# State chain of an RWKV-7 trunk layer: the solve's products on four 64 by 64 tiles and two PSUM banks, and the output norm's squares summed as two rounded parts

## The chip, the cores and the metric

One NeuronCore of one Trainium2 chip runs the whole kernel. The metric is the device time of one execution in microseconds (us), the median over several executions. Engine names are those of the profile: PE is TensorE's matmul stream, PEld its weight loads, DVE is VectorE, ACT is ScalarE, POOL is GpSimd, SP is SyncE, which here only issues DMAs.

## The reference

One layer of a hybrid decoder trunk over 1024 tokens of width 1024. The part that the change touches is the RWKV-7 branch: a recurrence over the tokens with one 64 by 64 state per head (16 heads), and a norm of its output per head.

```python
def rwkv7_scan(r, w, k, v, kk_neg, kk_a):
    def step(state, inp):
        rt, wt, kt, vt, an, bn = inp
        sa = jnp.einsum('bhvk,bhk->bhv', state, an)
        state = state * wt[:, :, None, :] + sa[..., None] * bn[:, :, None, :] + vt[..., None] * kt[:, :, None, :]
        yt = jnp.einsum('bhvk,bhk->bhv', state, rt)
        return state, yt
    ...
# in rwkv_branch:
    mu = jnp.mean(y, axis=-1, keepdims=True)          # over the 64 channels of a head
    var = jnp.mean(jnp.square(y - mu), axis=-1, keepdims=True)
    y = ((y - mu) * lax.rsqrt(var + LNX_EPS)).reshape(B, S, RWKV_WIDTH)
    y = y * ln_x_w.astype(f32) + ln_x_b.astype(f32)
    bonus = jnp.sum(rh * kh * r_k.astype(f32), axis=-1, keepdims=True) * vh
    y = y + bonus.reshape(B, S, RWKV_WIDTH)
    return y.astype(dt) * g
```

Around it stand one combined input projection, a pooling branch, cross-attention, three sigmoid gates that merge the branches, an output projection and a convolutional feed-forward layer.

## The kernel before

Everything is held with channels on the 128 partitions and tokens along the free axis. Large matrix products run as three passes over rounded parts: a float32 operand is split into a rounded high part (`fp32r`) and the rest, and `mm3` (lines 180 to 182) multiplies high by high, high by low and low by high, each a 128x128 weight against 128x512. Products of plain float32 operands are recorded as two passes each.

The recurrence is cut into 16 chunks of 64 tokens (`NCH = 16`, `C = 64`); the preceding stage solves each chunk's triangular system in 32 by 32 blocks and leaves the chunk's matrices in DRAM. The function `chain` then walks the chunks in order. Two heads stand on the 128 partitions (`lo` is partitions 0 to 63, `up` is 64 to 127), eight such pairs `i` make up the 16 heads. A chunk `c` has three visits to PE, and between them values go through DVE and ACT:

1. `pr`: 16 products of the state and the chunk's matrices, 64 columns each. DVE copies the result to `Rs` (line 800).
2. `py<-ring` (part of the output) and `pu`: `pu = nt * Rs` is the solve's product, 16 products of 64x64 by 64x64, head `lo` on rows and columns 0 to 63 and head `up` on 64 to 127, all into one bank. DVE copies the lower half of `pu` into `hv` (line 809) and ACT the upper half (line 810).
3. `ph` (the new state's increment) and `py<-rb` (the rest of the output), which read `hv`. DVE adds `ph` and the decayed state `Hd` into the next chunk's `hv` (line 828, two additions: `lo`, `up`), then into `Hn` (line 833); eight small ACT instructions scale `Hn` by the decay into `Hd` (line 835). ACT copies the output `py` out (line 836).

The next chunk's `pr` waits for both additions of line 828, so the chunks form one chain.

To keep PE busy while that chain passes through DVE and ACT, `visit` first emits *fill*: further steps of the input projection for the pooling, query and gate columns, three passes per step (`psg<-hh`). The table `fills`, here `279 + 121 * (v - 1) // 46`, says how many steps stand before visit `v`: two or three between any two visits. The scheduler orders each engine's instructions; `later` adds pure ordering between them.

Each block `b` of two chunks has 1024 by 128 outputs in `y`. `outputs(b - 1, n, ...)` finishes half of the block before, four channel groups at a time: squares on ACT (line 714), a sum over each head's 64 channels by one float32 product with a block matrix of ones (`pvar`, line 716), logarithm and exponential on ACT for the inverse root (`rstd`, line 214), and four DVE products and sums: by the inverse root, by `ln_w`, plus `gt[0]`, times `gt[1]` (lines 720 to 723). `gt[0]` and `gt[1]` are loaded from DRAM for each block by `gate`, and `store` writes the block. SP issues these and the loads of the next block's matrices (`ring`, `hv`, `pair`, `bk`, `rb`) from one queue.

PSUM has eight banks: the fill uses `psg` with tag `g1` (two), `psg` with tag `g0` (two) is idle in the chain, `py` and `pvar` share `pss` (two), and `bank` hands out `psc` and `psk` in turn to `pr`, `pu` and `ph`.

Of the kernel before, what the change touches and what calls it, by code (L numbers as in the profile page):

```python
# [9 lines left out]
F32 = mybir.dt.float32  # L10
FR = mybir.dt.float32r
AF = mybir.ActivationFunctionType
ALU = mybir.AluOpType
# [4 lines left out]
P = 128  # L18
# [3 lines left out]
C = 64  # L22
# [22 lines left out]
def trunk_kernel(ctx: ExitStack, tc: tile.TileContext, xT, memT, pvec, w_in, w_kv, w_upd, w_upg,  # L45
                 w_pool, w_ppool, w_pmem, w_prwkv, w_o, w_fup, w_fdn, out):
    nc = tc.nc
    V, A, G, PE, SP = nc.vector, nc.scalar, nc.gpsimd, nc.tensor, nc.sync
# [3 lines left out]
    psg = ctx.enter_context(tc.tile_pool(name="psg", bufs=2, space=PSUM))  # L52
# [11 lines left out]
    d_g = dtile([8, P, T], "d_g")  # L64
    d_bv = dtile([8, P, T], "d_bv")
# [23 lines left out]
    bonesr = const.tile([P, P], FR, name="bonesr")  # L89
# [5 lines left out]
    bones = bonesr.bitcast(F32)  # L95
# [122 lines left out]
    def rstd(dst, ps, eps_col, scale=1.0):  # L218
        act(dst, ps, AF.Ln, bias=eps[:, eps_col:eps_col + 1], scale=scale)
        act(dst, dst, AF.Exp, scale=-0.5)  # L220

    def later(i, ins, plain=False):

        tc.add_manual_dep(i if plain else i.ins, ins.name, nosync, reason="order")
# [13 lines left out]
    for k in range(KC):  # L238
        tag = ("X01", "X11", "HV", "HV")[k // 2]
# [116 lines left out]
    lr = lr_ctx.enter_context(tc.tile_pool(name="lr", bufs=1, side="right"))  # L356

    ld = lr.tile([P, T], FR, name="ld", tag="ld")
# [333 lines left out]
            dst = dst[:, :, n]  # L692
        SP.dma_start(dst.rearrange("c p t -> p c t"), src.rearrange("p (c u) s -> p c (u s)", u=2))

    gates, ready_y = {}, {}

    def gate(b):

        gates[b] = []
        for src, e in ((d_bv, "ld"), (d_g, "la")):  # L700
            gates[b].append(lr.tile([P, 8, 2 * C], F32, name="gt", tag=e))
            SP.dma_start(gates[b][-1], src[:, :, b * 2 * C:(b + 1) * 2 * C].rearrange("n p t -> p n t"))

    def store(b):

        SP.dma_start(d_y[:, :, b * 2 * C:(b + 1) * 2 * C].rearrange("n p t -> p n t"), ready_y[b])

    def outputs(b, n, q, after):

        y, gt = ready_y[b], gates[b]  # L710
        ln_w = pv[:, PV["ln_w"][0]:PV["ln_w"][0] + 8]
        ns = slice(n, n + 4)
        y_, q_ = y[:, ns], q.rearrange("p (n t) -> p n t", t=2 * C)
        A.activation(q_, y_, AF.Square)
        ps = pss.tile([P, 512], F32, name="pvar", tag="s")
        m = PE.matmul(ps, bones, q, start=True, stop=True)  # L716
        if after is not None:
            later(m, after)
        rstd(q, ps, 2, 1.0 / 64)
        V.tensor_tensor(y_, y_, q_, op=ALU.mult)  # L720
        V.tensor_tensor(y_, y_, ln_w[:, ns].unsqueeze(2).broadcast_to([P, 4, 2 * C]), op=ALU.mult)
        V.tensor_tensor(y_, y_, gt[0][:, ns], op=ALU.add)
        V.tensor_tensor(y_, y_, gt[1][:, ns], op=ALU.mult)

    def chain(fills):

        lo, up = slice(0, 64), slice(64, 128)
        ring = rw.tile([P, 2, 8, 3, 2 * C], F32, name="ring", tag="AR")
        pair = rw.tile([P, 2, 2, 8, 2 * C], F32, name="pair", tag="HV")
        state = rw.tile([P, 4, 8, C], F32, name="Rs", tag="NT")  # L730
        Rs, Hn, Hd = (state[:, n] for n in range(3))
        root = state[:, 3].rearrange("p n t -> p (n t)")
        held = {}

        due = []

        def load(b):

            ar, nt = ring[:, b % 2], pair[:, b % 2, 0]
            hv = rw.tile([P, 2, 8, 2, C], F32, name="hv", tag=f"X{b % 2}2")  # L740
            rb = rw.tile([P, 8, 2, 2 * C], F32, name="rb", tag=f"X{b % 2}1")
            bk = rw.tile([P, 8, 2, P], F32, name="bk", tag=f"X{b % 2}0")
            due.extend([(ar, d_ar[b].rearrange("p g i e t -> p (g i) e t")),
                        (hv[up, 0], d_hv[b, up].rearrange("p g i (u s) -> p (g i) u s", u=2)),
                        (hv[lo, 1], d_hv[b, lo].rearrange("p g i (u s) -> p (g i) u s", u=2)),
                        (nt, d_nt[b].rearrange("p g i t -> p (g i) t")),
                        (bk, d_bk[b].rearrange("p g i u s -> p (g i) u s")),
                        (rb, d_rb[b].rearrange("p g i e t -> p (g i) e t"))])
            held[b] = ar, nt, hv, rb, bk, pair[:, b % 2, 1]

        def send(n, after=None):

            while due and n:
                i = SP.dma_start(*due.pop(0))
                if after is not None:
                    later(i, after)
                n -= 1

        turn = [0]

        def bank(name):
            turn[0] ^= 1
            return (psc if turn[0] else psk).tile([P, 8, C], F32, name=name, tag="c" if turn[0] else "k")

        visits = [0]

        def visit(products, after):

            wide = fill_to(fills(visits[0]))
            visits[0] += 1  # L770
            for n, ((out_, l, r), kw) in enumerate(products):
                m = PE.matmul(out_, l, r, **kw)  # L772
                if n == 0:
                    later(m, wide)
                if after is not None:
                    later(m, after)
                after = m.ins
            send(1, after)
            return after

        ready = None
        for b in range(2):
            load(b)
            send(6)
        for c in range(NCH):
            b, u = divmod(c, 2)
            if u == 0 and 0 < b < NCH // 2 - 1:
                load(b + 1)
            ar, nt, hv, rb, bk, y = held[b]
            t = slice(u * C, (u + 1) * C)  # L790
            once = dict(start=True, stop=True)
            pr = bank("pr")
            py = pss.tile([P, 8, C], F32, name="py", tag="s")
            ke, ko = (up, lo) if c == 0 else (slice(0, P), slice(0, P))
            row = []
            for i in range(8):
                row.append(((pr[up, i], ar[ko, i, 2, t], hv[ko, 1, i, u]), once))
                row.append(((pr[lo, i], ar[ke, i, 0, t], hv[ke, 0, i, u]), once))
            visit(row, ready)
            made = V.tensor_copy(Rs, pr).ins  # L800
            pu = bank("pu")
            row = []
            for i in range(8 if c else 0):
                kw = dict(start=i == 0, stop=False)
                row.append(((py[lo, i], hv[lo, 0, i, u], ar[lo, i, 1, t]), kw))
                row.append(((py[up, i], hv[up, 1, i, u], ar[up, i, 1, t]), kw))
            row += [((pu[q, i], nt[q, i, t], Rs[q, i]), once) for i in range(8) for q in (lo, up)]
            last = visit(row, made)
            V.tensor_copy(hv[lo, 0, :, u], pu[lo])
            ready = A.copy(hv[up, 1, :, u], pu[up]).ins  # L810
            row = []
            if c + 1 < NCH:
                ph = bank("ph")
                for i in range(8):
                    row.append(((ph[up, i], bk[:, i, u, 64:128], hv[:, 1, i, u]), once))
                    row.append(((ph[lo, i], bk[:, i, u, 0:64], hv[:, 0, i, u]), once))
            for i in range(8):
                kw = dict(start=c == 0 and i == 0, stop=i == 7)
                row.append(((py[lo, i], hv[:, 0, i, u], rb[:, i, 0, t]), kw))
                row.append(((py[up, i], hv[:, 1, i, u], rb[:, i, 1, t]), kw))  # L820
            visit(row, ready)
            if c + 1 < NCH:
                hx = held[(c + 1) // 2][2]
                for q, e in ((lo, 0), (up, 1)):
                    if c == 0:
                        ready = V.tensor_copy(hx[q, e, :, 1 - u], ph[q]).ins
                    else:
                        ready = V.tensor_tensor(hx[q, e, :, 1 - u], ph[q], Hd[q], op=ALU.add).ins
                if c + 2 < NCH:
                    if c == 0:  # L830
                        V.tensor_copy(Hn, ph)
                    else:
                        V.tensor_tensor(Hn, ph, Hd, op=ALU.add)
                    for i in range(8):
                        A.activation(Hd[:, i], Hn[:, i], AF.Identity, scale=Dc[:, i, c + 1:c + 2])
            A.copy(y[:, :, t], py)
            ready_y[b] = y
            if b:
                outputs(b - 1, 4 * u, root, last)
            if u:  # L840
                if b:
                    store(b - 1)
                gate(b)
        for n in (0, 4):
            outputs(b, n, root, None)
        store(b)

    fill = [(j, spilled(d_zp[j])) for j in range(4)] + [(4 + j, spilled(d_zq[j])) for j in range(4)]
# [927 lines left out]
    last = [half_down(1, 0)]  # L1776
# [75 lines left out]
```

## Time and profile before

| | |
|---|---|
| median of 3 runs | 1952.37 us (1947.69, 1952.37, 1952.64) |
| the profiled execution | 1947.9 us, of which the span of its instructions is 1946.2 us |
| granted TensorE clock in it | 0.993 |
| busy share of the span | PE 97%, DVE 70%, ACT 54%, POOL 40% |
| the state chain | first `pr` at 666.0 us, the last chunk's `py` at 861.7 us |

The page counts the time in which an engine had an instruction running. A matmul's end is modelled, so matmul records overlap: a pass of the fill is recorded as 0.39 us but the next one starts about 0.23 us later, and what a group of passes costs PE is read from the starts. Rows of the time line merge neighbouring instructions of one kind; `x32` behind a group of small products are 16 products of two passes each. In brackets stands how long the engine had been idle, and what ended that.

### The profile page before, as it was taken

To read this page: it belongs to the slowest core of one execution; us is meant where nothing else is said; L and a number is where in the kernel's file an instruction comes from. 1 tells how busy PE (TensorE), PEld (TensorE's weight loads), DVE (VectorE), ACT (ScalarE), POOL (GpSimd) and SP (SyncE) were. 2 spreads that over 40 slices of the span, in tenths; PEclk is the share of its full clock that TensorE was granted. 3 is DMA by queue.
4 is the path that set the end of the run, shared out by engine and by line. 5 is a ranking of instruction groups with operands and counts; after the bars stand their busy time and mean duration, and the time that the engine had idled before them with its cause. 6 is when DMAs were issued, how large, how long until landed. Compare 5 with 4: busy or idle time off the path is not lost.

```text
span 1946.2 us, 33744 instructions
## 1 busy us (share of the span) xinstructions
PE 1886.9 (97%) x12204; PEld 1522.7 (78%) x12204; DVE 1356.7 (70%) x2022; ACT 1046.1 (54%) x2158; POOL 784.1 (40%) x867
## 2 busy tenths in 40 slices
PE   8999999999999999999999999999999999999997
PEld 6767777777777887778788888878788888888886
DVE  8677577677677345556964444679698888877798
ACT  7685385475474245455664344546554545454544
POOL 4422222222222211111323455556599889822441
PEclk9999999999999999999999999999999999999999
DMA  5326326335349669965336444653322222289775
GB/s 163 130 72 186 99 76 184 93 95 168 95 122 310 191 191 297 312 196 190 102 112 231 124 137 130 208 161 121 110 81 87 78 88 88 86 250 223 168 184 146
DMA packets 269639, 296.26 MB, mean 152 GB/s; under 512 B 18336, under 2 KB 219168, under 8 KB 266400
## 3 DMA queue, kind: packets, MB, share of 16 engines
q1 hardware_dynamic: 248480, 271.56, 44.8%
q0 software_dynamic: 11856, 14.16, 4.5%
q10 hardware_dynamic: 9136, 8.39, 1.4%
q8 instruction: 96, 1.57, 0.3%
q14 instruction: 71, 0.58, 0.1%
HBM read 207.00 MB, written 87.03 MB: 151 GB/s over the span
## 4 chain that ended last, share of the span: by engine, by line
PE 62%; DVE 5%; DMA 4%; issue 2%; ACT 2%; POOL 1%; ACTq 0%; POOLq 0%; DVEq 0%; SPq 0%
PE psg L180 10%; PE psg L182 10%; PE psg L181 10%; PE psf L182 6%; PE psf L180 6%; PE psf L181 6%; PE psd L181 2%; PE psd L182 2%; PE psd L180 2%; PE py L772 2%; PE pr L772 1%; DMA g<-d_zg 1%; PE ph L772 1%; PE pvar L716 1%; PE pu L772 1%
## 5 line engine op out<-in xcount | busy, mean ns | idle before, releaser
L139 POOL TENSOR_TENSOR wlo<-wraw,whi 128x256 fp32r<-128x256 f32 x464 | 403.0, 881 | 829.0 <-ACT whi L132 753.6
L180 PE MATMUL psg<-hh,whi 128*128 128x512 f32 x928 | 377.7, 407 | 12.4 <-ACT whi L132 9.0
L182 PE MATMUL psg<-hh,wlo 128*128 128x512 f32 x928 | 367.6, 397 | 1.8 <-POOL wlo L139 1.5
L181 PE MATMUL psg<-hl,whi 128*128 128x512 f32 x928 | 368.1, 397 | 0.7 <-DVE hl L266 0.6
L132 ACT CAST whi<-wraw 128x256 fp32r<-128x256 f32 x472 | 181.5, 403 | 246.8 <-PE psg L181 98.9
L180 PEld LDWEIGHTS psg<-hh,whi 128*128 128x128 f32 x928 | 174.8, 188 | 57.4 <-ACT whi L132 13.0
L182 PEld LDWEIGHTS psg<-hh,wlo 128*128 128x128 f32 x928 | 174.8, 188 | 44.1 <-POOL wlo L139 6.1
L181 PEld LDWEIGHTS psg<-hl,whi 128*128 128x128 f32 x928 | 175.0, 189 | 39.8 <-issue 4.3
L1178 POOL TENSOR_TENSOR wt<-a,wt 128x256 fp32r<-128x256 f32 x136 | 156.3, 1173 | 35.4 <-ACT wt L1177 35.2
L180 PE MATMUL psd<-f,u 128*128 128x512 f32 x292 | 113.3, 391 | 1.1 <-ACT f L1590 1.1
L181 PE MATMUL psd<-f,u 128*128 128x512 f32 x292 | 113.8, 390 | 0.5 <-DVE f L1594 0.5
L182 PE MATMUL psd<-f,u 128*128 128x512 f32 x292 | 113.6, 389 | 0.0
L182 PE MATMUL psf<-h2h,wt 128*128 128x512 f32 x272 | 105.9, 390 | 0.2 <-POOL wt L1178 0.2
L180 PE MATMUL psf<-h2h,wt 128*128 128x512 f32 x272 | 105.9, 389 | 0.1
L181 PE MATMUL psf<-h2l,wt 128*128 128x512 f32 x272 | 105.8, 389 | 0.0
L1192 DVE SCALAR_TENSOR_TENSOR d<-z,pv,d 128x1023 f32<-128x1023 f32 x68 | 101.1, 1491 | 2.2
L1178 POOL TENSOR_TENSOR wt<-s,wt 128x256 fp32r<-128x256 f32 x68 | 79.9, 1195 | 3.3 <-ACT wt L1177 2.0
L180 PE MATMUL psf<-t,wt 128*128 128x512 f32 x204 | 79.4, 389 | 0.0
L181 PE MATMUL psf<-t,wt 128*128 128x512 f32 x204 | 79.4, 389 | 0.0
L182 PE MATMUL psf<-t,wt 128*128 128x512 f32 x204 | 79.4, 389 | 0.0
L1190 ACT ACTIVATE d<-z,pv 128x1024 f32<-128x1024 f32 x34 | 42.4, 1248 | 65.8 <-DVE z L1272 50.1
L1177 ACT CAST wt<-a 128x256 fp32r<-128x256 f32 x136 | 50.7, 405 | 40.8 <-POOL wt L1178 28.1
(430 smaller groups left out, 4507.3 us busy)
## 6 DMA issues: line engine op xcount, KB each, us to landing
wraw<-in_w_in SPq DMA_DIRECT2D x176, 128.0 KB, 2.5
a<-in_w_fup SPq DMA_DIRECT2D x128, 128.0 KB, 2.4
d_ar<-AR SPq DMA_DIRECT2D x24, 512.0 KB, 4.2
d_zg<-st SPq DMA_DIRECT2D x48, 256.0 KB, 3.4
ring<-d_ar SPq DMA_DIRECT2D x8, 1536.0 KB, 10.8
wraw<-in_w_fup SPq DMA_DIRECT2D x80, 128.0 KB, 2.6
fraw<-d_f SPq DMA_DIRECT2D x33, 256.0 KB, 4.3
d_rb<-RB SPq DMA_DIRECT2D x16, 512.0 KB, 5.4
```

The source lines that it names most:

```text
L132: i = A.copy(hi, src)
L139: (V if lo_on_dve[0] else G).tensor_tensor(lo, src, hi.bitcast(F32), op=ALU.subtract)
L180: first = PE.matmul(ps, wh, xh, start=start, stop=False)
L181: PE.matmul(ps, wh, xl, start=False, stop=False)
L182: last_mm[0] = PE.matmul(ps, wl, xh, start=False, stop=stop).ins
L716: m = PE.matmul(ps, bones, q, start=True, stop=True)
L772: m = PE.matmul(out_, l, r, **kw)
L1177: A.copy(w[0][:, us], src[u])
L1178: low = eng.tensor_tensor(w[1][:, us], src[u], w[0][:, us].bitcast(F32), op=ALU.subtract)
L1190: A.activation(d, z, AF.Identity, scale=col("cw2", j), bias=col("cb", j))
L1192: V.scalar_tensor_tensor(d[:, n:], z[:, :T - n], col(cw, j), d[:, n:], op0=ALU.mult, op1=ALU.add)
```

## The change

Four things are changed in `chain` and its helpers.

- **The solve's products.** `pu` gets two banks instead of one (the next two turns of `bank`). Even `i` go to the first bank as before. For odd `i` the output half is swapped: head `lo` (rows 0 to 63) writes columns 64 to 127, head `up` writes columns 0 to 63, into the second bank. Four 64 by 64 tiles of the array are used in turn. DVE copies the first bank to `hv` in two copies of 64x256 (lines 820 and 821 of the changed kernel), ACT the second bank in two copies (lines 822 and 823).
- **The norm's sum.** `squared` makes the squares twice on ACT, once rounded into `sq[:, 0]` and once exactly into a PSUM tile `ysum`, and DVE subtracts to give the remainder `sq[:, 1]` (line 712). `outputs` sums them with two `fp32r` products (lines 722 and 725) instead of one float32 product. The inverse root stays in the PSUM tile.
- **Places.** The squares are written at the start of a chunk, and `outputs` between the copies of `pu` and the third visit, not at the end of the chunk. `Hn` moves from SBUF to a `psg` tile with tag `g0`, which `ysum` also uses.
- **Buffers.** `sq` takes the tag `ld` that held `gt[0]`; `gt[0]` takes the tag `la`, and `gt[1]` the part of `state` that held `Hn` and `root`. Hence it is printed as `Rs` in rows of the changed program.

```diff
     def gate(b):
-        gates[b] = []
-        for src, e in ((d_bv, "ld"), (d_g, "la")):
-            gates[b].append(lr.tile([P, 8, 2 * C], F32, name="gt", tag=e))
-            SP.dma_start(gates[b][-1], src[:, :, b * 2 * C:(b + 1) * 2 * C].rearrange("n p t -> p n t"))
+        gates[b] = lr.tile([P, 8, 2 * C], F32, name="gt", tag="la"), slot[0]
+        for gt, src in zip(gates[b], (d_bv, d_g)):
+            SP.dma_start(gt, src[:, :, b * 2 * C:(b + 1) * 2 * C].rearrange("n p t -> p n t"))
...
-    def outputs(b, n, q, after):
+    def squared(b, n, sq):
+        q = psg.tile([P, 512], F32, name="ysum", tag="g0")
+        for d in (sq[:, 0], q):
+            A.activation(d.rearrange("p (n t) -> p n t", t=2 * C), ready_y[b][:, n:n + 4], AF.Square)
+        V.tensor_tensor(sq[:, 1], q, sq[:, 0].bitcast(F32), op=ALU.subtract)
+        return q
+
+    def outputs(b, n, sq, q, after):
...
-        A.activation(q_, y_, AF.Square)
         ps = pss.tile([P, 512], F32, name="pvar", tag="s")
-        m = PE.matmul(ps, bones, q, start=True, stop=True)
+        m = PE.matmul(ps, bonesr, sq[:, 1], start=True, stop=False)
         if after is not None:
             later(m, after)
+        PE.matmul(ps, bonesr, sq[:, 0], start=False, stop=True)
         rstd(q, ps, 2, 1.0 / 64)
...
-        Rs, Hn, Hd = (state[:, n] for n in range(3))
-        root = state[:, 3].rearrange("p n t -> p (n t)")
+        Rs, Hd = (state[:, n] for n in range(2))
+        slot[0] = state[:, 2:4].rearrange("p a n t -> p (a n t)").rearrange("p (n t) -> p n t", n=8)
+        sq = lr.tile([P, 2, 512], FR, name="ysq", tag="ld")
...
+            if b:
+                q = squared(b - 1, 4 * u, sq)
             pr = bank("pr")
...
-            pu = bank("pu")
+            pu = [bank("pu") for _ in range(2)]
...
-            row += [((pu[q, i], nt[q, i, t], Rs[q, i]), once) for i in range(8) for q in (lo, up)]
+            row += [((pu[i % 2][o, i // 2], nt[q, i, t], Rs[q, i]), once) for i in range(8)
+                    for q, o in ((lo, up if i % 2 else lo), (up, lo if i % 2 else up))]
             last = visit(row, made)
-            V.tensor_copy(hv[lo, 0, :, u], pu[lo])
-            ready = A.copy(hv[up, 1, :, u], pu[up]).ins
+            V.tensor_copy(hv[lo, 0, 0::2, u], pu[0][lo, :4])
+            V.tensor_copy(hv[up, 1, 0::2, u], pu[0][up, :4])
+            A.copy(hv[lo, 0, 1::2, u], pu[1][up, :4])
+            ready = A.copy(hv[up, 1, 1::2, u], pu[1][lo, :4]).ins
+            if b:
+                outputs(b - 1, 4 * u, sq, q, last)
...
                 if c + 2 < NCH:
+                    Hn = psg.tile([P, 8, C], F32, name="Hn", tag="g0")
...
             ready_y[b] = y
-            if b:
-                outputs(b - 1, 4 * u, root, last)
...
         for n in (0, 4):
-            outputs(b, n, root, None)
+            outputs(b, n, sq, squared(b, n, sq), None)
```

Line numbers behind the change are 10 to 16 higher than before. The instruction order moves at two places.

On PE, from `pu` of a chunk in the middle of the chain to `ph`, before (the six fill passes between are shown by the first and the last):

```order
L772 MATMUL py<-ring,hv 64x64 x16
L772 MATMUL pu<-Rs,pair 64x64 x16
L180 MATMUL psg<-hh,whi 128x512
...
L182 MATMUL psg<-hh,wlo 128x512
L716 MATMUL pvar<-Rs,bonesr 128x512
L772 MATMUL ph<-hv,bk 64x64 x16
```

and now:

```order
L780 MATMUL py<-ring,hv 64x64 x16
L780 MATMUL pu<-Rs,pair 64x64 x16
L722 MATMUL pvar<-ysq,bonesr 128x512
L725 MATMUL pvar<-ysq,bonesr 128x512
L180 MATMUL psg<-hh,whi 128x512
...
L182 MATMUL psg<-hh,wlo 128x512
L780 MATMUL ph<-hv,bk 64x64 x16
```

The sum of the squares stands directly behind `pu`, ahead of the fill; in the other chunks before it stood behind `py<-rb`. The numbers of fill passes between the visits are as before but for an exchange of three passes between neighbouring places in a few chunks; a middle chunk has 24.

On DVE, one chunk before, from the copy of `pr` on:

```order
L800 COPY Rs<-pr 128x512
L809 COPY hv<-pu 64x8x64
L828 TENSOR_TENSOR hv<-ph,Rs 64x8x64 x2
L833 TENSOR_TENSOR Rs<-ph,Rs 128x512
L720 TENSOR_TENSOR pair<-pair,Rs 128x512
L721 TENSOR_TENSOR pair<-pair,pv 128x512
L722 TENSOR_TENSOR pair<-pair,gt 128x512
L723 TENSOR_TENSOR pair<-pair,gt 128x512
```

and one chunk now (`ysum` holds the inverse root; the second `Rs` in `L730` is `gt[1]`, in `L843` it is `Hd`):

```order
L810 COPY Rs<-pr 128x512
L820 COPY hv<-pu 64x4x64
L821 COPY hv<-pu 64x4x64
L727 TENSOR_TENSOR pair<-pair,ysum 128x512
L728 TENSOR_TENSOR pair<-pair,pv 128x512
L729 TENSOR_TENSOR pair<-pair,gt 128x512
L843 TENSOR_TENSOR hv<-ph,Rs 64x8x64
L730 TENSOR_TENSOR pair<-pair,Rs 128x512
L843 TENSOR_TENSOR hv<-ph,Rs 64x8x64
L849 TENSOR_TENSOR Hn<-ph,Rs 128x512
L712 TENSOR_TENSOR ysq<-ysum,ysq 128x512
```

The four steps of the output norm stood behind both additions to `hv`; now three of them stand ahead of the first addition and one between the two. This is the order of four of the thirteen chunks that have both (call it order X, chunks 3, 5, 11 and 13, counted from 0). In seven chunks two stand ahead of the first addition and one between (order Y), in two chunks one ahead and one between (order Z). On ACT the copies of `pu`, then the logarithm and the exponential (line 214) follow each other; in every second chunk, the first of each block, one square (line 711) stands between logarithm and exponential.

More of the change, by code (lines that the diff above doesn't have):

```diff
@@ L693, in spill @@
         SP.dma_start(dst.rearrange("c p t -> p c t"), src.rearrange("p (c u) s -> p c (u s)", u=2))
-    gates, ready_y = {}, {}
+    gates, ready_y, slot = {}, {}, [None]
     def gate(b):
-        gates[b] = []
-        for src, e in ((d_bv, "ld"), (d_g, "la")):
-            gates[b].append(lr.tile([P, 8, 2 * C], F32, name="gt", tag=e))
-            SP.dma_start(gates[b][-1], src[:, :, b * 2 * C:(b + 1) * 2 * C].rearrange("n p t -> p n t"))
+        gates[b] = lr.tile([P, 8, 2 * C], F32, name="gt", tag="la"), slot[0]
+        for gt, src in zip(gates[b], (d_bv, d_g)):
+            SP.dma_start(gt, src[:, :, b * 2 * C:(b + 1) * 2 * C].rearrange("n p t -> p n t"))
     def store(b):
         SP.dma_start(d_y[:, :, b * 2 * C:(b + 1) * 2 * C].rearrange("n p t -> p n t"), ready_y[b])
-    def outputs(b, n, q, after):
+    def squared(b, n, sq):
[5 more added lines that the diff above has]
+    def outputs(b, n, sq, q, after):
         y, gt = ready_y[b], gates[b]
```

## The prediction

> **What bounds the kernel now.** I read the page first, then the busy time by stretches, then the time line of one chunk, and last the groups by shape for durations.
>
> ```profile
> span 1946.2 us, 33744 instructions
> PE 1886.9 (97%) x12204; PEld 1522.7 (78%) x12204; DVE 1356.7 (70%) x2022; ACT 1046.1 (54%) x2158; POOL 784.1 (40%) x867
> ```
>
> The profiled execution took 1947.9 us, 1.7 us more than this span. The median shown, 1952.37 us, is 4.5 us above it; of the three runs shown one is at its level (1947.69). I make the sum against 1947.9 and carry the difference over to the median.
>
> Busy time in three stretches of the state chain (window; length, then PE, PEld, DVE, ACT, POOL with counts, granted clock, DMA share, GB/s):
>
> ```profile
> 740.00:765.00 25.00, 25.00 (x380) 19.18 (x380) 12.21 (x18) 13.78 (x35) 3.71 (x5) 1.00 1.01 319
> 765.00:790.00 25.00, 25.00 (x404) 19.87 (x404) 12.05 (x18) 12.59 (x33) 2.73 (x5) 1.00 0.96 305
> 790.00:815.00 25.00, 25.00 (x413) 20.07 (x408) 13.79 (x20) 13.32 (x34) 3.61 (x5) 1.00 0.95 302
> ```
>
> PE has no gap in 75 us, while DVE and ACT are about half busy. The clock is full. So in the chain a chunk costs what PE has to do, and a pass taken from PE is time taken from the span, as long as the path through DVE and ACT stays under cover of the fill. DMA is the other resource near its end.
>
> One chunk on the time line (start, duration, engine, instruction):
>
> ```profile
> 757.02 1.15 PE L772 MATMUL pr<-hv,ring 128*64 128x64 f32 x32
> 758.10 0.50 PE L180 MATMUL psg<-hh,whi 128*128 128x512 f32 x1
> 758.44 0.40 PE L181 MATMUL psg<-hl,whi 128*128 128x512 f32 x1
> ...
> 760.04 0.39 PE L182 MATMUL psg<-hh,wlo 128*128 128x512 f32 x1
> 760.26 0.68 DVE L800 COPY Rs<-pr 128x512 f32<-128x512 f32 x1
> 760.36 1.15 PE L772 MATMUL py<-ring,hv 64*64 64x64 f32 x32
> 761.34 1.10 PE L772 MATMUL pu<-Rs,pair 64*64 64x64 f32 x32
> 762.37 0.50 PE L180 MATMUL psg<-hh,whi 128*128 128x512 f32 x1
> 762.49 0.68 DVE L809 COPY hv<-pu 64x512 f32<-64x512 f32 x1 [1.55 <-PE pu L772]
> 763.21 0.58 ACT L810 COPY hv<-pu 64x512 f32<-64x512 f32 x1 [2.56 <-DVE hv L809]
> 763.64 0.39 PE L182 MATMUL psg<-hh,wlo 128*128 128x512 f32 x1
> 763.87 1.02 PE L716 MATMUL pvar<-Rs,bonesr 128*128 128x512 f32 x2
> 764.82 1.15 PE L772 MATMUL ph<-hv,bk 128*64 128x64 f32 x32
> ...
> 766.08 1.39 DVE L828 TENSOR_TENSOR hv<-ph,Rs 64x512 f32<-64x512 f32 x2 [2.90 <-PE ph L772]
> 769.13 1.15 PE L772 MATMUL pr<-hv,ring 128*64 128x64 f32 x32
> ```
>
> From `pr` to `pr` are 12.11 us. A fill pass costs 0.23 us (758.44 to 760.04 are seven), a group of 32 small passes 0.98 us when another of its kind follows (760.36 to 761.34). Behind a group the first fill pass costs 0.34 us (758.10 to 758.44). The additions to `hv` end at 767.47, while `pr` starts at 769.13: 1.7 us of slack, which is what the change can use up.
>
> **The solve's products.** There are 16 chunks of 32 passes:
>
> ```profile
> L772 PE MATMUL pu<-Rs,pair x512: 218/218/267, 678.9 to 858.4; 64*64 64x64 f32 x171
> L716 PE MATMUL pvar<-Rs,bonesr x32: 590/592/697, 706.2 to 870.4; 128*128 128x512 f32 x32
> ```
>
> A pass lasts 218 ns and the group 1.10 us, so 0.88 us lie between its first and its last start. Head `lo` and head `up` use different tiles and run as a pair, so these are 15 steps of 0.059 us, or 0.94 us for 16. With four tiles in turn there are 8 steps, 0.47 us, if the four run at once. Whether they do, no row shows for this shape. The nearest rows are these of the stage before, 32 by 32 tiles; in the second group two products that use four different tiles between them overlap at their border:
>
> ```profile
> 230.01 1.20 PE L672 MATMUL pz<-tb,NT 32*32 32x32 f32 x64
> 231.14 0.50 PE L502 MATMUL psu<-ld,uhi 128*128 128x512 f32 x1
> ...
> 234.30 0.19 PE L672 MATMUL pz<-tb,NT 32*32 32x32 f32 x1
> 234.31 0.19 PE L680 MATMUL pw<-NT,tb 32*32 32x32 f32 x1
> 234.31 0.22 PE L672 MATMUL pz<-tb,NT 32*32 32x32 f32 x2
> 234.34 0.19 PE L680 MATMUL pw<-NT,tb 32*32 32x32 f32 x1
> ```
>
> 64 passes in 1.13 us are 18 ns each, so passes can be issued faster than the 29 ns of `pu`; and `pz`, later in the program, starts while passes of `pw` are still starting, so a pass in another tile does not queue behind them. What is new in `pu` is that two row halves deliver to the same 64 columns, in different banks. That is seen in the products of the matrices, 64 rows by 128 columns:
>
> ```profile
> 157.88 2.06 PE L601 MATMUL ps<-AR,BK 64*128 64x128 f32 x32
> 162.64 3.84 PE L601 MATMUL ps<-AR,BK 64*128 64x128 f32 x32 [1.82 <-ACT RB L605]
> ```
>
> The same 32 passes take once 2.06, once 3.84 us, as if the halves ran together the first time and in turn the second. So the saving lies between 0.47 us a chunk and nothing (halves in turn, but the two heads of each bank still as a pair, as today). Below nothing I exclude, since that pair is today's. I take 0.47, nearer to the undisturbed row: 16 x 0.47 = 7.5 us.
>
> [...]
>
> **The norm's sum.** `pvar` (x32, so 16 sums of two passes) stands between the last fill pass at 763.64 and `ph` at 764.82. Without it, such a group follows a fill pass after 0.32 us (760.04 to 760.36). It costs 1.18 - 0.32 = 0.86 us; two `fp32r` passes cost 0.46. Saved: 16 x 0.40 = 6.4 us, bounded by 0 if they were no faster than the float32 passes.
>
> **What is added elsewhere.** By shape, in the chain (the two 256 wide ones from the stage before):
>
> ```profile
> L722 DVE TENSOR_TENSOR pair<-pair,gt 128x512 f32<-128x512 f32 x15 | 12.1, 808 | 1.8 <-DMA gt<-d_bv 1.3
> L721 DVE TENSOR_TENSOR pair<-pair,pv 128x512 f32<-128x512 f32 x15 | 11.6, 774 | 0.4
> L809 DVE COPY hv<-pu 64x512 f32<-64x512 f32 x16 | 10.9, 681 | 26.3 <-PE pu L772 26.3
> L606 DVE TENSOR_TENSOR NT<-ps,mstrict 64x256 f32<-64x256 f32 x32 | 13.3, 416 | 24.0 <-ACT RB L605 23.7
> L605 ACT COPY RB<-ps 128x256 f32<-128x256 f32 x32 | 11.9, 372 | 0.1
> L714 ACT ACTIVATE Rs<-pair 128x512 f32<-128x512 f32 x16 | 10.1, 630 | 6.3 <-DVE pair L720 6.2
> L214 ACT ACTIVATE Rs<-pvar,eps 128x512 f32<-128x512 f32 x16 | 11.0, 689 | 6.3 <-PE pvar L716 6.3
> ```
>
> DVE gets one subtraction (0.69) and 2 x 0.42 for 0.68 in copies, ACT one square (0.63) and 2 x 0.37 for 0.58: 0.8 us a chunk each, on engines half busy. The two engines' copies now run side by side (today ACT waits for DVE, 763.21), and `ph`, behind nine or six fill passes, covers them. `Hn` in PSUM I cost as its SBUF form, 0.69; its cover is the whole fill ahead of the next additions. The gate loads are the same two on SP, with the same loads queued behind.
>
> What counts is the place of the output steps. Estimated from `pu`'s start with nine passes to `ph` and six to `pr`: `pvar` at 0.6, fill at 1.1, `ph` at 3.3, its result at 4.5, `pr` due at 6.9. ACT: copies to 1.5, logarithm to 2.2, square to 2.8 in the first chunk of a block, exponential to 2.8 or 3.5. Order X, on second chunks: the three steps on DVE to 3.6, 4.4, 5.2; first addition to 5.9, step to 6.6, second addition to 7.3: `pr` is 0.5 late. Order Y on first chunks: two steps to 5.0, addition 5.7, step 6.5, addition 7.2: 0.35 late. With nine passes to `pr` (due at 7.6), neither is. That makes chunks 3 and 5 at 0.5, 13 (seven passes) at 0.25, and 4, 12 and 14 at 0.35: 2.3 us. `Rs` then follows at about 10, ahead of the next `pu` at 11.2.
>
> Sum: -7.5 - 6.4 + 2.3 = -11.6 us. Behind the chain the order of instructions is the same but for the first steps, so the gain is carried on. Against the profiled execution 1936.3, against the median shown 1940.8; I forecast 1941 us.
>
> **Rivals.**
>
> *Only two tiles at once* (the slow row of L601). `pu` wins nothing, the chunk is 0.47 longer, which also takes in the lateness of `pr`: -6.4 + 0.3, 1946.3 us. For it speaks that collapse; against it the border of `pw` and `pz`. Chance 0.15. [...]
>
> *Output steps eat the gain.* Lateness of `pr` is 2.3 us only if the steps last 0.7 to 0.8. Single ones took 1.1 us (a row of the time line; below it a gate load with its median time to landing, and the longest wait for one):
>
> ```profile
> 856.52 1.10 DVE L723 TENSOR_TENSOR pair<-pair,gt 128x512 f32<-128x512 f32 x1
> gt<-d_bv SPq DMA_DIRECT2D x5, 512.0 KB, 6.1
> DVE pair L723 <- DMA gt<-d_g: 1.6, 1, 1.6
> ```
>
> A gate load that lands late would now hold up an addition, which it does not today; I estimate a distance of 8.9 us from the last output step of a block to the first use of the next load (`pu` + 7.4 to the next `pu` + 5.1), against 6.1 for the load and about 1 for its issue. If half of the thirteen chunks lose 1 us more, 6 to 7 us go and the time is 1947, within the bound of no change. Chance 0.17.
>
> *Slower.* The same place, but with the load late in each of the seven first chunks: each us beyond the 2 us that it has to spare goes straight to `pr`. It decides at 2 us of lateness in each (14 us, the whole gain); at 3 us it costs 21 - 11.6, 1962 us. For it speaks DMA at a share of 0.95 to 1.01 and 8% less time for the same bytes; against it that one such wait lasted 1.6 us in the whole chain. Chance 0.12.
>
> DMA as a bound by itself: 319 GB/s at a share of 1.01 against 305 x 12.1 / 11.2 = 330 wanted, so a chunk could not fall below 11.6: about 8 us gained, 1945. I count it as the lower end of the forecast case, since the share counts packets that wait for each other.
>
> **How the numbers follow.** The forecast case has 0.56: 1945 (DMA) to 1935 (lateness none, and the lower level of the runs shown). With two tiles 0.15, eaten 0.17, slower 0.12. The range 1934 to 1950 leaves out the slower case and a little at the low end. About 0.3%, 5.9 us, is what a measurement of this kernel can tell from no change. Faster by more: the forecast case and half of the two-tile case, 0.62; within: the rest of it and the eaten case, 0.25; slower 0.13.
>
> **What would show it.** `pu` to the next matmul 0.56 instead of 1.03 us; the two passes of `pvar` 0.23 to 0.34 apart; chunks near 11.2 us; a few waits of PE `pr` for DVE `hv` of under 0.6 us each. Wrong if `pu` keeps 1.0 us, or if `pr` waits for DVE in most chunks, with `gt` loads named before L729.

## The result, and the profile after

The changed kernel takes 1933.76 us (median of six runs, 1933.04 to 1936.65); the kernel before, beside it, 1948.46 (six runs, 1947.69 to 1952.64). The ratio is 0.9921, 95% interval 0.9908 to 0.9934. A second measurement gave 1935.12 against 1950.08, ratio 0.9926, 0.9908 to 0.9943. So about 15 us are gained, where 11.6 were forecast; the profiled execution took 1933.07 us.

The page of the changed kernel, span and engines:

```profile
span 1931.4 us, 33821 instructions
PE 1869.7 (97%) x12204; PEld 1515.9 (78%) x12204; DVE 1366.2 (71%) x2054; ACT 1048.7 (54%) x2190; POOL 785.7 (41%) x867
```

PE has the same 12204 passes and is busy 17.2 us less. The same three stretches of the chain (columns as before):

```profile
740.00:765.00 25.00, 24.70 (x409) 19.89 (x408) 16.00 (x26) 15.10 (x45) 3.78 (x4) 1.00 1.02 314
765.00:790.00 25.00, 24.75 (x440) 20.06 (x438) 13.43 (x23) 13.64 (x39) 2.94 (x4) 1.00 1.01 302
790.00:815.00 25.00, 24.36 (x390) 19.68 (x381) 14.89 (x24) 14.80 (x40) 2.93 (x4) 1.00 1.06 337
```

PE still carries the chain, but is no longer full: 1.2 us of these 75 are gaps. The DMA engines moved 337 GB/s in the third stretch, more than the 319 of the kernel before. One chunk on the time line:

```profile
744.06 1.09 PE L780 MATMUL py<-ring,hv 64*64 64x64 f32 x30
744.93 0.27 PE L780 MATMUL pu<-Rs,pair 64*64 64x64 f32 x2
744.98 0.22 PE L780 MATMUL py<-ring,hv 64*64 64x64 f32 x2
745.04 0.63 PE L780 MATMUL pu<-Rs,pair 64*64 64x64 f32 x30
745.60 0.51 PE L722 MATMUL pvar<-ysq,bonesr 128*128 128x512 f32 x1
745.72 0.42 DVE L820 COPY hv<-pu 64x256 f32<-64x256 f32 x1 [3.06 <-PE pu L780]
745.78 0.37 ACT L822 COPY hv<-pu 64x256 f32<-64x256 f32 x1 [2.66 <-PE pu L780]
745.94 0.39 PE L725 MATMUL pvar<-ysq,bonesr 128*128 128x512 f32 x1
746.17 0.40 PE L180 MATMUL psg<-hh,whi 128*128 128x512 f32 x1
...
747.64 1.15 PE L780 MATMUL ph<-hv,bk 128*64 128x64 f32 x32
...
751.92 1.15 PE L780 MATMUL pr<-hv,ring 128*64 128x64 f32 x32
```

`py` and `pu` together, from the first start to the next matmul, take 1.54 us (744.06 to 745.60); before they took 2.01 (760.36 to 762.37). That is 0.47 a chunk. A pair of `pu` starts before the last pair of `py`. The two passes of `pvar` start 0.34 apart, and the fill follows 0.23 later. The copies of `pu` start on the two engines 0.05 us apart. This `pr` comes 11.2 us after the one at 740.7 (before: 12.11).

What PE waited for from 600 to 900 us (total, times, longest):

```profile
PE pmm L934 <- issue: 2.8, 1, 2.8
...
PE pr L780 <- DVE hv L843: 0.6, 1, 0.6
PE pr L780 <- issue: 0.6, 2, 0.3
PE pr L780 <- DMA hv<-d_hv: 0.2, 1, 0.2
```

`pr` waits in a few chunks, for 1.4 us by this view. A gap of 2.8 us ahead of `pmm`, the product of the memory norm that follows the chain, is longer than before (1.6, and 1.8 in a second profile of before).

The next table cuts each profile into stretches, worked out from the starts of PE's instructions: first `pr`; from there to the last fill pass ahead of `pmm` ("chain"); waits in the chain, which are what the steps before `pr`, `ph` and `pu` take above their usual 0.32 (0.04 for `pu`); from the last fill pass to `pmm`; `pmm` to the first product with `mh`, the normed memory; from there to the end. All in us; two values are two profiles of one kernel.

| kernel | median | ratio to before (95%) | first `pr` | chain | waits in it | to `pmm` | `pmm` to `mh` | rest |
|---|---|---|---|---|---|---|---|---|
| before | 1948.46 | | 666.0, 667.9 | 220.03, 220.02 | 0.1, 0.1 | 2.0, 2.2 | 3.07, 3.07 | 1055.0, 1053.2 |
| changed | 1933.76, 1935.12 | 0.9921, 0.9926 | 665.6, 668.9 | 206.69, 206.03 | `pr` 1.9, 0.9 | 3.2, 4.1 | 4.63, 4.46 | 1051.2, 1052.0 |
| e1 | 1943.12 | 0.9964 (0.9953 to 0.9975) | 668.9 | 214.07 | `ph` 1.8 | 1.8 | 3.06 | 1053.5 |
| e2 | 1947.07 | 0.9982 (0.9972 to 0.9992) | 668.4 | 216.63 | `pr` 3.4, `ph` 0.3 | 3.4 | 4.62 | 1051.5 |
| e3 | 1943.00 | 0.9962 (0.9948 to 0.9977) | 666.5 | 213.31 | `pr` 1.0 | 3.3 | 4.53 | 1051.6 |
| e5 | 1941.84 | 0.9964 (0.9950 to 0.9978) | 668.6 | 215.31 | `ph` 8.4 | 2.0 | 2.81 | 1051.3 |
| e6 | 1933.28 | 0.9910 (0.9897 to 0.9923) | 668.1 | 204.75 | 0.0 | 3.3 | 4.61 | 1051.0 |
| e7 | 1929.73 | 0.9889 (0.9874 to 0.9903) | 667.7 | 202.40 | `pr` 2.7 | 3.3 | 4.61 | 1050.2 |
| e8 | 1932.20 | 0.9918 (0.9898 to 0.9938) | 668.2 | 204.83 | `pu` 2.6, `ph` 0.3 | 3.6 | 3.01 | 1048.1 |
| e9 | 1926.82 | 0.9882 (0.9865 to 0.9898) | 667.3 | 202.05 | `pu` 2.3 | 0.2 | 3.60 | 1053.3 |
| e10 | 1935.59 | 0.9926 (0.9910 to 0.9942) | 668.6 | 206.44 | `pr` 1.4, `pu` 0.2 | 0.6 | 3.56 | 1054.4 |

The chain repeats to 0.01 us where it does not wait (before). The stretches ahead of it and behind it, nearly the same code in all rows, differ by 1 to 3 us between profiles of one kernel. So the chain column carries the arguments below, and the medians only differences of more than about 3 us.

One thing has to be taken out of that column first: it doesn't hold the same number of fill passes in every row. They are 508 before and in e1, 505 in the changed kernel, e2, e3 and e6 to e8, 510 in e5, 504 in e9 and e10. At 0.23 us a pass, 0.7 us of what the changed kernel gains in the column are three passes that now stand behind `pmm`. The gain that is left is 12.6 us in the first pair of profiles and 13.3 in the second.

### The profile page after: what moved, and what is told of

It reads as the page before. It is cut to its first block, busy times and chain, and to the rows that moved or that the text cites. A ratio compares the mean times of both kernels' runs of the same rounds, so it can differ in the third digit from the quotient of the medians.

```text
span 1931.4 us, 33821 instructions
## 1 busy us (share of the span) xinstructions
PE 1869.7 (97%) x12204; PEld 1515.9 (78%) x12204; DVE 1366.2 (71%) x2054; ACT 1048.7 (54%) x2190; POOL 785.7 (41%) x867
## 3 DMA queue, kind: packets, MB, share of 16 engines
q8 instruction: 96, 1.57, 0.3%
## 4 chain that ended last, share of the span: by engine, by line
PE 65%; DVE 5%; DMA 3%; ACT 1%; issue 1%; POOL 0%; SPq 0%; DVEq 0%; ACTq 0%; POOLq 0%
PE psg L180 11%; PE psg L182 11%; PE psg L181 11%; PE psf L182 6%; PE psf L180 6%; PE psf L181 6%; PE psd L181 3%; PE psd L182 3%; PE psd L180 3%; PE py L780 1%; DMA R<-d_f 1%; PE pr L780 1%; PE ph L780 1%; DMA hv<-d_hv 1%; DMA gt<-d_bv 1%
```

## Experiments

**e1, the products alone.** The kernel before with four tiles, two banks and four copies; the norm untouched.

```diff
-            pu = bank("pu")
+            pu = [bank("pu") for _ in range(2)]
...
-            row += [((pu[q, i], nt[q, i, t], Rs[q, i]), once) for i in range(8) for q in (lo, up)]
+            row += [((pu[i % 2][o, i // 2], nt[q, i, t], Rs[q, i]), once) for i in range(8)
+                    for q, o in ((lo, up if i % 2 else lo), (up, lo if i % 2 else up))]
...
```

> The kernel before with the solve's products alone changed: four tiles, two banks, two copies each on DVE and ACT; the norm's sum, its place and the buffers as before. Theory (PE bound chain, each pass that starts earlier is span): pu to the next matmul falls from 1.03 to 0.56 us in all 16 chunks, 7.5 us less than before, no wait of pr. Rival (part of the 14.7 us comes from the place of the output steps or from the end of the chain): the same 7.5 us, so the two halves of the change would not add up to 14.7. Rival (side by side copies shorten the chain through DVE and ACT): nothing from that here, since pr does not wait before either.

The chain took 214.07 us, 5.96 less than before, with one new kind of wait in it:

```profile
PE ph L772 <- DVE hv L811: 1.6, 2, 1.2
```

Without its 1.8 us of waits (0.1 before) the products save 5.96 + 1.7 = 7.7 us, 0.48 a chunk; 7.5 was the term of the sum. The wait of `ph` was not expected: without the norm's change the output steps stand behind the additions of one chunk, so ahead of the next chunk's copies of `pu`. In both chunks where they hold these copies up, something else had come late first. ACT's copy of `py` waited for a store of outputs from the same tile, for 3.38 us ahead of the one and 2.95 ahead of the other. The inverse root is queued behind that copy on ACT, and the output steps wait for the root.

**e2, the norm alone.** The changed kernel with `pu` back on two tiles in one bank.

```diff
-            pu = [bank("pu") for _ in range(2)]
+            pu = bank("pu")
...
-            row += [((pu[i % 2][o, i // 2], nt[q, i, t], Rs[q, i]), once) for i in range(8)
-                    for q, o in ((lo, up if i % 2 else lo), (up, lo if i % 2 else up))]
+            row += [((pu[q, i], nt[q, i, t], Rs[q, i]), once) for i in range(8) for q in (lo, up)]
...
```

> The changed kernel with pu back on two tiles and one bank; squares in two parts, the place of the outputs, Hn in PSUM and the gate buffers as in the changed kernel. Theory: 16 x 0.40 = 6.4 us less than before, minus little waiting at pr since a chunk is 0.47 us longer. Rival (the earlier place of the outputs wins at the end of the chain): 8 to 10 us less, with the extra gained behind the last py, where the changed kernel was 2.4 us further ahead at its last pvar than at its last py.

The chain is 3.40 us shorter, not 6.4, since it waits:

```profile
PE pr L780 <- issue: 2.4, 4, 0.6
PE pr L780 <- DVE hv L840: 0.5, 2, 0.3
```

With 3.7 us of waits taken out (0.1 before), and 0.7 for the three fill passes fewer, the norm's part is 6.3 us, 0.39 a sum (0.40 was the term). The changed kernel against e1, worked out the same way, gives 6.8 in its first profile and 6.5 in its second. The one part makes the other's waits: on ACT the undivided copy of `pu` stands between the logarithm and the exponential, and in chunk 5 the first output step starts 2.7 us behind the start of `pvar`, against 2.1 in the changed kernel. So the steps that the change puts ahead of the additions cost more than in the whole change.

**e3, two banks but two tiles.** The changed kernel with its banks and its copies, but each row half keeps its own columns.

```diff
-            row += [((pu[i % 2][o, i // 2], nt[q, i, t], Rs[q, i]), once) for i in range(8)
-                    for q, o in ((lo, up if i % 2 else lo), (up, lo if i % 2 else up))]
+            row += [((pu[i % 2][q, i // 2], nt[q, i, t], Rs[q, i]), once) for i in range(8) for q in (lo, up)]
...
```

> The changed kernel with the output halves of odd products not swapped: two banks and the four copies stay, but only two tiles of the array are used. Theory (tiles, not banks): pu goes back to 0.88 us from first to last start, the kernel is 7 us slower than the changed one (less what pr no longer waits, up to 2), 7 to 9 us faster than before. Rival (the banks and the copies side by side are what pays): same time as the changed kernel, 14.7 us less than before.

The chain took 213.31 us, 6.6 more than the changed kernel's first profile, 7.5 with the waits taken out of both. Time line of a chunk:

```profile
747.84 1.15 PE L780 MATMUL py<-ring,hv 64*64 64x64 f32 x32
748.82 1.10 PE L780 MATMUL pu<-Rs,pair 64*64 64x64 f32 x32
749.85 0.51 PE L722 MATMUL pvar<-ysq,bonesr 128*128 128x512 f32 x1
```

`pu` is back at 1.03 us to the next matmul, and no pass of it starts among those of `py`. So the four tiles bring the 0.47, and the banks and copies by themselves nothing. Four tiles in one bank were not tried, so whether the second bank is needed stays open.

**e5, the output steps in the old place.** The changed kernel, `outputs` called again at the end of the chunk.

```diff
-            if b:
-                outputs(b - 1, 4 * u, sq, q, last)
             row = []
...
             ready_y[b] = y
+            if b:
+                outputs(b - 1, 4 * u, sq, squares, last)
```

> The changed kernel with outputs back at the end of the chunk (the squares stay at its start), so that on DVE both additions to hv stand ahead of the output steps. Theory: the six waits of pr of the changed kernel (1.9 us in all) go, the rest stays: about 2 us faster than the changed kernel, 16 to 17 us less than before. Rival (the earlier place wins at the end of the chain): slower than the changed kernel by 1 to 3 us.

This expectation was wrong: the kernel is 7 us faster than before, not 16 to 17, and its chain is 8.6 us longer than the changed kernel's (1.2 of them are five more fill passes). The waits of PE, and what ACT and DVE did ahead of the longest of them:

```profile
PE ph L780 <- DVE hv L821: 7.4, 5, 3.1
```

```profile
828.16 0.59 ACT L850 COPY pair<-py 128x512 f32<-128x512 f32 x1 [5.17 <-DMA d_y<-pair]
...
831.50 0.69 DVE L727 TENSOR_TENSOR pair<-pair,ysum 128x512 f32<-128x512 f32 x1 [2.92 <-ACT ysum L214]
832.53 0.69 DVE L712 TENSOR_TENSOR ysq<-ysum,ysq 128x512 fp32r<-128x512 f32 x1 [0.34 <-ACT ysum L711]
833.14 1.11 DVE L728 TENSOR_TENSOR pair<-pair,pv 128x512 f32<-128x512 f32 x1
834.28 1.09 DVE L729 TENSOR_TENSOR pair<-pair,gt 128x512 f32<-128x512 f32 x1
835.41 0.69 DVE L730 TENSOR_TENSOR pair<-pair,Rs 128x512 f32<-128x512 f32 x1
...
836.44 0.43 DVE L821 COPY hv<-pu 64x256 f32<-64x256 f32 x1
837.01 1.15 PE L780 MATMUL ph<-hv,bk 128*64 128x64 f32 x32 [3.10 <-DVE hv L821]
```

The four steps and the new subtraction come in one row on DVE, and the copies of `pu`, which `ph` needs, come behind all five. The order on DVE is not the only cause. Here, and ahead of two more of the seven waits of `ph`, ACT's copy of `py` had waited 3.0 to 5.2 us for a store, which made the inverse root late; no run changes the store alone. So the new place of `outputs`, which the prediction counted as a cost, is what keeps the two savings together: it costs 0.9 to 1.9 us of waits of `pr` and avoids 8.4 of `ph`.

**r_before and r_after, the two kernels again.**

> The kernel before again, unchanged, for a second profile. The time from the chain's first product to its last fill pass should come out again as 220.0 us within 0.5, since in it the tensor engine waits 0.1 us in all. The stretch from the memory norm's product to the end was 2.2 us longer in the first profile than in the changed kernel's. If that is jitter between executions, it comes out 1 us or more shorter here; if it belongs to the change, it stays.

> The changed kernel again, unchanged, for a second profile and for a time beside the next two on one chip. The chain's first product to its last fill pass: 206.7 us, with 1 to 3 us of waits of pr in it, perhaps in other chunks than 4, 6, 10 and 11. Against the kernel before: 14 to 16 us faster.

The chain came out as before to 0.01 us, and 0.7 shorter for the changed kernel, with 1.0 less of waits; those that are left stand ahead of chunks 4, 6 and 12. The rest behind `mh` was 1.8 us shorter in the second profile of before, so what the first comparison had there is jitter between executions. From first `pr` to the end the two profiles give 1280.2 and 1278.5 before, 1265.7 and 1266.6 after: 13.2 us on average, where the medians say 14.7 and 15.0.

**e6, the four steps behind the additions.** The product and the inverse root stay where the change puts them.

```diff
-        V.tensor_tensor(y_, y_, q_, op=ALU.mult)
+
+    def gated_out(b, n, q, after):
...
+        m = V.tensor_tensor(y_, y_, q_, op=ALU.mult)
+        if after is not None:
+            later(m, after)
...
                         ready = V.tensor_tensor(hx[q, e, :, 1 - u], ph[q], Hd[q], op=ALU.add).ins
+                if b:
+                    gated_out(b - 1, 4 * u, squares, ready)
...
```

> The changed kernel with the norm's product and rstd where the change puts them, and the four VectorE steps behind it emitted only after the additions that the next chunk waits for. If the waits of pr come from these four steps standing ahead of the additions, the six gaps of 0.37 to 1.02 us before pr go to the usual 0.32: 1.9 us less up to the last fill pass (204.8 instead of 206.7), and no new wait of ph, as the copies of pu stand ahead of the steps again. Rival: the last of the four steps now stands between the copy of Rs and those of pu, and ph waits for them as it does in the kernel with the steps in the old place; then the time stays or grows by 1 to 5 us.

As expected: 204.75 us, and in 300 us of trace PE waits for none of `pr`, `ph` and `pu`. So the waits of `pr` hang on the steps ahead of the additions, the one that passed on a late gate load (next section) among them. Eight middle chunks in a row last 11.2 us each. The median cannot tell it from the changed kernel.

**e7, `py` on four tiles too.**

```diff
-            py = pss.tile([P, 8, C], F32, name="py", tag="s")
+            py = [pss.tile([P, 8, C], F32, name="py", tag="s") for _ in range(2)]
...
+                o, x = (up, lo) if i % 2 else (lo, up)
+                row.append(((py[i % 2][o, i // 2], hv[lo, 0, i, u], ar[lo, i, 1, t]), kw))
+                row.append(((py[i % 2][x, i // 2], hv[up, 1, i, u], ar[up, i, 1, t]), kw))
```

> The changed kernel with the other products of 64 by 64 treated alike: py from ring in two banks with swapped halves for every second head, so that it too runs on four tiles; pvar goes into the bank of ysum, and y is copied in three pieces. If four tiles halve any set of 32 such passes that now takes 0.88 us, 15 chunks give 15 x 0.40 = 6.0 to 15 x 0.47 = 7.1 us more: the stretch to the last fill pass 199.6 to 200.7, less 0 to 2 us more of waits of pr, since chunks get shorter and VectorE's row of work does not. Rival: in the changed kernel the first passes of pu already run beside the last of py, so the set of py costs less than 0.88, and the gain is under 3 us.

The time line of a chunk, and the waits of PE:

```profile
743.90 0.69 PE L780 MATMUL py<-ring,hv 64*64 64x64 f32 x32
744.42 0.65 PE L780 MATMUL pu<-Rs,pair 64*64 64x64 f32 x32
745.00 0.50 PE L722 MATMUL ysum<-ysq,bonesr 128*128 128x512 f32 x1
```

```profile
PE pr L780 <- DVE hv L845: 1.4, 1, 1.4
...
PE py L780 <- DMA rb<-d_rb: 0.8, 1, 0.8
...
```

`py` and `pu` now take 1.10 us together instead of 1.54. The chain is 202.40, or 199.7 without its waits, against 204.8 to 205.1 for the changed kernel without its own: 5.1 to 5.4 us gained. A wait of `py` for the load of `rb`, 0.8 us once, is still in it; without that it is 5.9 to 6.2, of 6.0 to 7.1 expected. Longer waits of `pr` take 0.8 to 1.8 us of it back. With 1929.73 us this beats both kernels.

**e8 and e9, both together, and then less fill in the chain; e10, the changed kernel with less fill in the chain.** The edit of e9 and e10:

```diff
-    chain(lambda v: 279 + 121 * (v - 1) // 46 if v else 262)
+    chain(lambda v: 279 + 116 * (v - 1) // 46 if v else 262)
...
-        covered = fill_to(424)
+        covered = fill_to(430)
```

The first line takes 15 fill passes out of the chain; the second raises the number of fill steps that `pmm` has to stand behind. In the traces 105 passes stand between the last `py` and `pmm`, 91 in the changed kernel.

> Steps late and py on four tiles together. py on four tiles alone brought 206.0 to 202.4 to the last fill pass, with 2.7 us of waits of pr in it, so 199.7 without them; steps late alone took the waits away altogether. If both hold, 199.5 to 200 here and no wait of pr, about 3 us less than with py on four tiles alone: near 1926.5. Rival: with shorter chunks the additions themselves come too late, behind the copies and not behind the four steps; then 1 us or more of waits stays.

> The kernel of e8 with five of the fill's steps (15 passes, 3.4 us of them) moved from among the chain's products to behind the chain, ahead of the memory norm's product. The tensor engine's gap ahead of that product falls from 3.3 to about 0 to 0.5 us, and the passes behind it run at 0.23 us instead of 0.43 for eight of them (1.6 us). With fewer passes as cover the chain's own waits may come back. Without them 4 to 5 us less than e8; rival: the chain waits for VectorE by what was taken away (3 us), and the time is that of e8.

> The changed kernel with the same five steps of the fill moved behind the chain, and nothing else. If the slow passes behind the memory norm's product (0.43 us instead of 0.23, six to eight of them) come from the gap of more than 3 us ahead of it, they are all at 0.23 here, as in the kernel before, whose gap was 2.0 us. First product of the memory norm to the first product of its projection: 3.1 us instead of 4.6. Gap 0 to 1 us. In all 4 to 5 us less than the changed kernel if the chain does not wait more; its waits of pr were 0.9 to 1.9 us and may grow to 3. Rival: the slow passes come from the chain's end as such (the order of the work there) and stay whatever the gap.

e8 did not reach 1926.5. Its chain took 204.83 us; `pr` does not wait, but in one chunk `pu` does, for 2.3 us, and eight slow fill passes behind that wait (last section) cost 1.6 more. ACT and DVE there (brackets: idle before, and what ended it):

```profile
796.61 0.37 ACT L867 COPY pair<-py 128x256 f32<-128x256 f32 x1 [5.67 <-DMA d_y<-pair]
...
798.29 0.69 DVE L712 TENSOR_TENSOR ysq<-ysum,ysq 128x512 fp32r<-128x512 f32 x1 [3.56 <-ACT ysum L711]
798.89 1.19 DVE L738 TENSOR_TENSOR pair<-pair,gt 128x512 f32<-128x512 f32 x1
800.01 0.68 DVE L819 COPY Rs<-pr 128x512 f32<-128x512 f32 x1
```

The first of ACT's three copies of `py` waited 5.67 us for a store. So the square behind them is late; the subtraction waits for it on DVE, and the copy of `Rs`, which `pu` needs, is queued behind that subtraction. In e6 the same wait for the store was 2.41 us, in a longer chunk, and DVE came to the same subtraction without idle time. Both waits of `pu` in e9 follow the same wait of ACT (5.63 and 3.98 us). e9 took 1926.82 us and has the lowest ratio, but its interval overlaps with that of e7, and its chain (202.05, with 2.3 us of waits of `pu`) is that of e7: whether it beats e7 is open.

In e9 and e10 the gap ahead of `pmm` is gone, as expected, and no pass behind `pmm` is slow. Counted from the first `pr`, `pmm` comes 2.9 and 3.1 us earlier in e10 than in the two profiles of the changed kernel. Yet e10's median is the changed kernel's, not 4 to 5 us lower as expected: the rest behind `mh` is the longest of all but one. So far as the medians tell, the gap ahead of `pmm` was no loss that filling it could win back. Of the 3 us, 0.7 are three more fill passes in the rest; where the others are lost again, within a rest that varies by 2 us anyway, the profiles don't settle.

## Why the prediction was right and wrong

*The four tiles: right.* 0.48 a chunk where 0.47 was forecast, and the rival with two tiles at once falls with e3. Before, the two passes of a pair start 0.007 us apart into one bank, and the next pair 0.058 behind them; in the change four passes start within 0.010 us, every 0.058. In e7 the 32 passes of `py` start in 0.52 us up to the next group (743.90 to 744.42), 16 ns each.

*The slow row that spoke for two tiles: misread.* The same 32 passes of `L601` took 2.06 and then 3.84 us, which the prediction read as row halves in turn. The granted clock (third column from the end) says otherwise:

```profile
157.88:159.86 1.98, 1.98 (x33) 1.86 (x32) 0.00 (x0) 1.95 (x5) 0.00 (x0) 1.00 0.55 182
162.64:166.41 3.77, 3.67 (x33) 3.18 (x33) 3.23 (x8) 2.31 (x9) 0.73 (x1) 0.57 0.02 6
```

At 0.57 of the clock, 3.77 us are worth 2.15 at full rate. The halves need not have changed their order at all, so that rival had no row for it.

*The norm's sum: right.* 6.3 to 6.8 us instead of 6.4, 0.39 to 0.43 a sum instead of 0.40.

*The waits of `pr`: right kind, too large, and the total near by luck.* The term was 2.3 us, and 1.9 and 0.9 were measured. By its own mechanism, steps ahead of the additions, it is 0.9 in both profiles: order X held up `pr` behind chunks 3 and 5 by 0.38 to 0.40 each (0.5 forecast) and behind 11 and 13 by 0.15 at most, and order Y, forecast at 0.35 in three chunks, made no wait by itself. The other 1.0 us of the first profile are loads: 0.3 for one of `hv`, and 0.7 for a gate load, the mechanism of the rival on the slower side.

```profile
794.04 0.68 DVE L843 TENSOR_TENSOR hv<-ph,Rs 64x512 f32<-64x512 f32 x1
796.19 0.69 DVE L729 TENSOR_TENSOR pair<-pair,gt 128x512 f32<-128x512 f32 x1 [1.47 <-DMA gt<-d_bv]
796.91 0.69 DVE L843 TENSOR_TENSOR hv<-ph,Rs 64x512 f32<-64x512 f32 x1
```

`L729` waited 1.47 us for its load, the second addition behind it came late, and `pr` by 0.7 us. At `pr` this shows in one chunk of one profile; that rival needed 2 us in each of seven.

*DMA as a bound: did not come.* Chunks lasted 11.2 us, under the 11.6 that this bound allowed, and 337 GB/s were moved in the third stretch, above the 330 that such a chunk was reckoned to need.

*Copies and other additions: right.* 0.42 on DVE and 0.37 on ACT for half a bank, as the nearest rows had it, and they hide.

*What failed.* The forecast lies 7.2 us above the result, and two steps made that. The first is the step that carries the sum from the profiled execution to the median shown, 1952.37, a median of three runs of which two lay high. Six runs, these three among them, have it at 1948.46: 3.9 us. From the level of the profile, 1947.9, the prediction's own sum gives 1936.3. The second is the sum itself, 11.6 for 14.7 in these medians. The chain's part of it was 12.6 and 13.3 us in the two profiles, so 1.0 to 1.7 us of the 3.1 lie there: the term for the waits of `pr` was too large by 0.4 to 1.4, and the products and the norm make up the rest within 0.6. The other 1.4 to 2.1 us lie outside the chain, where the sum let the gain be carried on unchanged. That is less than what those stages vary by from one execution to the next, and has no cause shown. And one reading was wrong: the new place of the output steps was counted as a cost of 2.3 us alone, while e5 shows that the old place, with the rest of the change, costs 8.4 us of waits.

## What to carry to other kernels

Products of 64 by 64 on both row halves took about half the time here when every second one delivered to the other column half in a second bank (`py` and `pu` together 1.10 us in e7, where they took 2.01 before); look for all sets of that shape, as e7 did. When PE's groups get shorter, read the DVE order for what stands ahead of the copy or addition that the next group needs: time taken from PE was only kept here where that order let it through (e5 has 8.4 us of waits of `ph`). Then follow the late step one engine further: in e1, e8 and e9, and in part of e5's waits, it began at a copy on ACT that waited for a store, for 2.95 to 5.67 us. When stretches of two kernels are compared, count the instructions in them first. And a median of three runs that lie 5 us apart passes that uncertainty on to a forecast of the time: later medians of the kernel before, over 11 to 23 runs, are 1949.62 to 1951.55.

## What the hardware showed

The fill passes behind `pmm` slowed down behind the longer gap. The changed kernel, and then the second profile of before:

```profile
875.52 0.87 PE L934 MATMUL pmm<-msq,ones 128*128 128x256 f32 x2 [2.81 <-issue]
...
877.05 0.63 PE L180 MATMUL psg<-hh,whi 128*128 128x512 f32 x1
877.47 0.63 PE L181 MATMUL psg<-hl,whi 128*128 128x512 f32 x1
```

```profile
890.11 0.67 PE L920 MATMUL pmm<-msq,ones 128*128 128x256 f32 x2 [1.78 <-issue]
...
891.54 0.39 PE L182 MATMUL psg<-hh,wlo 128*128 128x512 f32 x1
891.77 0.39 PE L180 MATMUL psg<-hh,whi 128*128 128x512 f32 x1
```

They start 0.43 us apart instead of 0.23, for three to seven passes. This came in six of the seven profiles in which PE had been idle for 2.8 to 3.7 us ahead of `pmm`, and in none of the six with 1.8 us or less. The seventh, e8, had it inside the chain, behind the wait of `pu`:

```profile
800.74 1.13 PE L789 MATMUL pu<-Rs,pair 64*64 64x64 f32 x32 [2.25 <-DVE Rs L819]
...
802.82 0.63 PE L180 MATMUL psg<-hh,whi 128*128 128x512 f32 x1
803.25 0.63 PE L181 MATMUL psg<-hl,whi 128*128 128x512 f32 x1
```

There eight passes from 802.82 on start 0.43 us apart. The granted clock was 0.50 around all these passes. The changed kernel, with the columns of the stretches of the chain:

```profile
872.45:875.86 3.41, 0.60 (x5) 0.34 (x3) 2.45 (x6) 2.52 (x8) 1.92 (x3) 1.00 0.44 152
875.86:879.28 3.42, 3.42 (x10) 2.68 (x9) 1.67 (x4) 1.99 (x5) 0.83 (x2) 0.50 0.80 214
```

In the clock record of each trace, half rate starts and ends on steps of 3.41 us: in the changed kernel it lasted from 312.66 to 316.08, from 595.97 to 599.38 and from 875.86 to 879.28, and these starts lie 83 and 82 such steps apart. Around the slow passes it lasted one step in six of the seven profiles and two in e8, from 800.24 to 807.06 us. Counted by these steps, PE was idle for 2.1 to 3.3 us of the one ahead of each of the seven falls. The longer gaps without a fall lie across a border: 3.2 us ahead of `pmm` in e8 as 1.9 and 1.3, and 3.1 us ahead of `ph` in e5 as 1.1 and 2.0. So in these traces it counted where a gap fell, and not only how long it was. Over the whole traces of the kernel before and of the changed one, from 40 us on, PE was idle for 1.57 to 3.18 us of each of the 11 steps at full rate ahead of half rate, and for at most 1.53 us of every other step at full rate.
